# Seven block products in place of eight for six of 22 pairs of feature tiles in the down projections of a two-layer encoder

## The chip, the cores and the metric

The kernel runs on one core of a Trainium2 chip. The metric is the device time of one execution in microseconds. The profile is one execution, recorded by the hardware profiler; its rows give the time of each instruction on each engine: PE (TensorE, matmuls), DVE (VectorE), ACT (ScalarE), POOL and SP (the queue that issues DMAs).

## The reference

Two layers over 256 tokens of width 2048. Each layer has a token mixer (attention) and a gated channel mixer, each between two RMS norms, with a residual: x = x + norm_post(f(norm_pre(x))). All in float32. The part that matters here is the channel mixer:

```python
u = h @ w_up                                  # 256 x 2048 by 2048 x 11264
gate = depthwise_conv3(u[..., :5632]) + b
return (gelu(gate) * u[..., 5632:]) @ w_down  # 256 x 5632 by 5632 x 2048
```

The last product is the down projection. It runs twice, once per layer.

## The kernel before

**Numbers in two parts.** Every float32 operand of a matmul is kept as a high and a low part in the type fp32r. A product of two tiles is three matmuls, high by high, high by low and low by high (`mm3`, lines 172 to 174). The stationary operand holds 128 features by 128 tokens, the moving one 128 features by 512 outputs.

**Weights.** All weights are one list of tiles of 128 x 1024 (512 KB), in the order of their use (`all_chunks`); a tile of a down projection holds two feature tiles by 512 outputs, so the 44 feature tiles make 22 pairs. `_load` (line 103) fetches a tile through SP's DMA queue into one of four buffers, `_split` makes its parts: ScalarE copies into `whi` (line 117), VectorE subtracts into `wlo` (line 118); each of these has three buffers. `weights()` is called once for each tile as its products are issued: it splits two tiles ahead and loads three further.

**The down projection.** `out_proj` (the part ahead of line 364) goes through four groups of 512 outputs. In a group, `proj_tok` sums 22 weight tiles into two PSUM banks, one per half of 128 tokens; one weight tile is an item of 12 matmuls (2 halves x 2 feature tiles x 3). After a group, ScalarE squares and sums each half (line 282) for the norm, and VectorE multiplies it by the gain into `m` (line 350). The last group keeps back three weight tiles (`HOLD`) and finishes the first half of the tokens before the second, so that the first half's part of what follows can begin: `factor` (lines 374 to 379) forms each token's factor, `add` (line 383) adds the result to the residual `x`; in layer 0, transposes (line 405), dummy matmuls (`warm`, line 156) and the splitting of the new x for the next mixer follow, and in layer 1 the output transfers (line 396). In front of the down projection, the last group of the up projection is evacuated by lines 247, 248, 922, 923, 511 and 512 on ScalarE and VectorE; `gh` and `gl` hold the 44 feature tiles in two parts.

**What sets the order.** The kernel is written as a sequence with generators: `now(gen)` queues small pieces, `tick()` after each item issues one piece of each, `finish(gen)` issues the rest at once. The builder (a framework that puts in all waits) then gives each engine one fixed sequence, in which an instruction that it expects to be held up can be put behind a later one; instructions that write the same PSUM bank keep their order. On the chip each engine runs its sequence in order.

**Buffers by tag.** Tiles `xm0` to `xm3` hold the split x in the up projection (a quarter of the 16 feature tiles each, in this order) and later `m`.

## Time and profile before

| | us |
|---|---|
| runs (median of 3, lowest, highest) | 2072.59, 2072.4, 2081.38 |
| the profiled execution's own time | 2072.57 |
| its span, first to last instruction | 2070.8 |
| up projection of layer 0 (a stretch of it) | 560 to 820 |
| down projection of layer 0 | 823.05 to about 1062.6 |
| down projection of layer 1 | to about 2062.8 |

A row of the timeline is: start in us, duration in us, engine, line of the kernel, operation, output<-input, shapes, count; in brackets the idle time before it and what ended it. Matmuls are pipelined, so one of 389 ns can be followed by the next much sooner: the distance of two starts is the cost. The span is 1.8 us shorter than the execution's time.

### The profile page before, as it was taken

Reading aid. Unit: us, or ns where it says so; the run is one execution under the profiler, and the core shown is the slowest. Engines: PE = TensorE matmul, PEld = TensorE weight load, DVE = VectorE, ACT = ScalarE, POOL = GpSimd, SP = SyncE. Lnnn points to the kernel's source line nnn. Section 1 sums busy time; section 2 is a strip of 40 time slices with the busy share of each in tenths; the row PEclk is TensorE's granted clock in tenths of the full one; section 3 lists DMA queues with packets and bytes.
Section 4 is the critical chain, followed back from the end, with each engine's and each line's share of the span. In section 5 each row is a group of like instructions: output and inputs, shape, how many; then the busy total and the mean of one; then the engine's idle time right before and its main releaser. Section 6 shows DMA issues by size and latency. Waiting matters only on the chain.

```text
span 2070.8 us, 28951 instructions
## 1 busy us (share of the span) xinstructions
PE 2057.9 (99%) x10977; PEld 1764.1 (85%) x10977; DVE 1340.6 (65%) x2051; ACT 1084.6 (52%) x1695; POOL 0.2 (0%) x4
## 2 busy tenths in 40 slices
PE   9999999999999999999999999999999999999998
PEld 7888888888888888888888998888888888888886
DVE  6877757667667667444466875666766766754444
ACT  6655546555555555344455654555555555544443
POOL 0000000000000000000000000000000000000000
PEclk9999999999999999999999999999999999999999
DMA  8545565666666666666665445566666666666664
GB/s 315 176 153 163 164 200 174 186 193 190 188 192 191 187 192 190 196 198 199 198 186 170 125 129 177 177 188 190 185 195 191 188 191 190 185 200 198 198 194 154
DMA packets 108716, 385.96 MB, mean 186 GB/s; under 512 B 12064, under 2 KB 12576, under 8 KB 108576
## 3 DMA queue, kind: packets, MB, share of 16 engines
q1 hardware_dynamic: 108288, 383.83, 60.6%
q8 instruction: 86, 1.41, 0.3%
q14 instruction: 54, 0.44, 0.1%
q10 hardware_dynamic: 288, 0.28, 0.0%
HBM read 381.96 MB, written 2.10 MB: 185 GB/s over the span
## 4 chain that ended last, share of the span: by engine, by line
PE 98%; DVE 1%; ACT 0%; DMA 0%; issue 0%; DVEq 0%; SPq 0%
PE ps L186 31%; PE ps L172 16%; PE ps L174 16%; PE ps L173 16%; PE ps L187 16%; PE ps L463 1%; PE ps L242 1%; DVE x L383 1%; PE ps L405 0%; DMA raw<-in_w_in 0%; PE ps L790 0%; DVE wlo L118 0%; ACT junk L282 0%; PE ps L238 0%; DVE xhl L517 0%
## 5 line engine op out<-in xcount | busy, mean ns | idle before, releaser
L118 DVE TENSOR_TENSOR wlo<-raw,whi 128x1024 fp32r<-128x1024 f32 (+1 forms) x710 | 867.9, 1223 | 672.1 <-ACT whi L117 670.4
L117 ACT CAST whi<-raw 128x1024 fp32r<-128x1024 f32 (+1 forms) x710 | 745.9, 1052 | 786.5 <-PE ps L174 417.5
L186 PE MATMUL ps<-xhl,whi 128*128 128x512 f32 x2816 | 978.6, 394 | 1.0 <-DVE xhl L517 1.0
L187 PE MATMUL ps<-xhl,wlo 128*128 128x256 f32 x2816 | 779.2, 277 | 0.0
L186 PEld LDWEIGHTS ps<-xhl,whi 128*128 128x128 f32 x2816 | 527.6, 188 | 123.2 <-DVE xhl L517 1.9
L187 PEld LDWEIGHTS ps<-xhl,wlo 128*128 128x128 f32 x2816 | 528.7, 188 | 1.1 <-DVE wlo L118 0.5
L172 PE MATMUL ps<-whi,gh 128*128 128x512 f32 x704 | 273.9, 389 | 0.0
L174 PE MATMUL ps<-whi,gl 128*128 128x512 f32 x704 | 273.9, 389 | 0.0
L173 PE MATMUL ps<-wlo,gh 128*128 128x512 f32 x704 | 273.9, 389 | 0.0
L174 PEld LDWEIGHTS ps<-whi,gl 128*128 128x128 f32 x704 | 132.2, 188 | 27.7
L173 PEld LDWEIGHTS ps<-wlo,gh 128*128 128x128 f32 x704 | 132.2, 188 | 27.4
L172 PEld LDWEIGHTS ps<-whi,gh 128*128 128x128 f32 x704 | 132.2, 188 | 27.1
L172 PE MATMUL ps<-whi,xhl 128*128 128x512 f32 x352 | 138.8, 396 | 1.3 <-ACT whi L117 1.2
L173 PE MATMUL ps<-wlo,xhl 128*128 128x512 f32 x352 | 137.6, 391 | 0.0
L174 PE MATMUL ps<-whi,xhl 128*128 128x512 f32 x352 | 137.1, 391 | 0.0
L172 PE MATMUL ps<-whi,oh 128*128 128x512 f32 x256 | 100.0, 390 | 0.0
L173 PE MATMUL ps<-wlo,oh 128*128 128x512 f32 x256 | 99.7, 389 | 0.0
L174 PE MATMUL ps<-whi,ol 128*128 128x512 f32 x256 | 99.6, 389 | 0.0
L247 ACT COPY half<-ps 128x256 f32<-128x256 f32 x176 | 65.0, 369 | 45.6 <-PE ps L186 36.0
L172 PEld LDWEIGHTS ps<-whi,xhl 128*128 128x128 f32 x352 | 66.0, 188 | 15.1 <-ACT whi L117 1.5
L174 PEld LDWEIGHTS ps<-whi,xhl 128*128 128x128 f32 x352 | 66.0, 188 | 13.9
L173 PEld LDWEIGHTS ps<-wlo,xhl 128*128 128x128 f32 x352 | 66.3, 188 | 13.4 <-DVE wlo L118 0.9
(186 smaller groups left out, 1584.9 us busy)
## 6 DMA issues: line engine op xcount, KB each, us to landing
raw<-in_w_up SPq DMA_DIRECT2D x352, 512.0 KB, 4.1
raw<-in_w_down SPq DMA_DIRECT2D x176, 512.0 KB, 4.2
raw<-in_w_in SPq DMA_DIRECT2D x88, 512.0 KB, 3.8
raw<-in_w_out SPq DMA_DIRECT2D x64, 512.0 KB, 3.9
gb<-in_post SPq DMA_DIRECT2D x16, 256.0 KB, 3.9
raw<-in_w_qn SPq DMA_DIRECT2D x8, 512.0 KB, 3.6
raw<-in_w_kn SPq DMA_DIRECT2D x8, 512.0 KB, 3.6
raw<-in_w_v SPq DMA_DIRECT2D x8, 512.0 KB, 3.6
```

The source lines that it names most:

```text
L117: self.nc.scalar.copy(hi[:, s], raw[:, s])
L118: self.nc.vector.tensor_tensor(out=lo[:, s], in0=raw[:, s], in1=hi[:, s].bitcast(F32), op=ALU.subtract)
L172: mm(ps, lh, rh, start=start, stop=False)
L173: mm(ps, lh, rl, start=False, stop=False)
L174: mm(ps, ll, rh, start=False, stop=stop)
L186: mm(out[i], hi[:, s], x(k), start=k == 0, stop=False)
L187: mm(out[i][:, :T], lo[:, s], x(k)[:, :T], start=False, stop=k == nk - 1)
L242: self.tc.keep_in_program_order(self.nc.tensor.transpose(out, x, self.ident))
L247: self.nc.scalar.copy(b, ps[:, T:])
L383: return nc.vector.scalar_tensor_tensor(out=x, in0=m[c][:, t, s], scalar=r[t], in1=x, op0=ALU.mult, op1=ALU.add)
L463: nc.tensor.matmul(ps[:, i, :], l, r, start=n == 0, stop=n == len(pairs) - 1))
```

## The change

`ffn` calls a new function `down` in place of `out_proj`. It goes through the outputs in two halves of 1024 (two blocks of 512) in place of four groups of 512, so four PSUM banks take the sums of a half (two blocks by two token halves). Of the 22 pairs of feature tiles, 16 are done as before ("plain"), an item for each block. The first six pairs go by the Strassen-Winograd rule: two token halves, two feature tiles and two output blocks are a 2 x 2 by 2 x 2 block product, done with seven block products in place of eight. They come in four items (steps 0 to 3 with 2, 2, 2 and 1 products); the order of a half is four plain items, then for each such pair the steps 0, plain, 1, 2, plain, 3, plain, then the remaining ten plain items.

- Products that are shared between outputs go into four further PSUM banks. After the sixth pair `added` combines them, and `total` adds the result to the plain banks.
- The token sums of the rule (`sums` in `down`) are made on VectorE from the two parts of the tokens, in three blocks of two pairs, and split again. They use `xm3` as scratch and `xm0` to `xm2` for the results; the split x now sits in `xm0`, `xm1`, `xm3`, `xm2` in this order. What of them is not yet issued is issued ahead of the first step 0.
- The weight sums (`Seven.sums`) are four subtractions on VectorE for each pair and half, in place, issued right behind the split of step 0. Steps 0 and 1 split the one tile before and after, step 2 the other, step 3 a half tile.
- `passage` is the former end of `out_proj`; for the down projection `total` of the last block comes ahead of the squares there.

The diff, cut:

```diff
--- before.py
+++ after.py
...
+XM = 0, 1, 3, 2
+PAIRS = 6
+PLAIN0 = 4
+def down_order():
+    plain = [("plain", p, o) for o in range(2) for p in range(PAIRS, KF // 2)]
+    out, plain = plain[:PLAIN0], deque(plain[PLAIN0:])
+    for p in range(PAIRS):
+        for j in (0, None, 1, 2, None, 3, None):
+            out.append(plain.popleft() if j is None else ("seven", p, j))
+    return out + list(plain)
+class Seven:
+    def __init__(self, a, b):
+        self.srcs, self.raw = (a, b), None
+    def load(self, model):
+        if self.raw is None:
+            self.raw = []
+            for src, tag in zip(self.srcs, "ab"):
+                raw = model.room.tile([P, 1024], F32, tag=f"seven_{tag}", name=f"seven_{tag}", bufs=1)
+                model.nc.sync.dma_start(out=raw, in_=src)
+                self.raw.append(raw)
+    def step(self, model, j):
+        a, b = self.raw
+        return (a, a, b, self.t2)[j] if j else a
+    def sums(self, model):
+        nc = model.nc
+        a, b = self.raw
+        self.t2 = model.room.tile([P, 512], F32, tag="seven_t", name="seven_t", bufs=1)
+        a0, a1, b0, b1 = a[:, :512], a[:, 512:], b[:, :512], b[:, 512:]
+        for out, x, y in ((a0, b0, a0), (self.t2, b1, a0), (a1, a1, self.t2), (b0, b1, b0)):
+            nc.vector.tensor_tensor(out=out, in0=x, in1=y, op=ALU.subtract)
...
+        if isinstance(self.chunks[i], tuple):
+            self.chunks[i][0].load(self)
+            self.loaded[i] = None
+            return
...
         raw = self.loaded.pop(i)
+        seven, step = self.chunks[i] if raw is None else (None, 0)
+        if seven:
+            raw = seven.step(self, step)
         hi = self.wp.tile([P, 1024], F32R, tag="whi", name="whi", bufs=3)
         lo = self.wp.tile([P, 1024], F32R, tag="wlo", name="wlo", bufs=3)
-        n = 1024 // parts
+        n = raw.shape[-1] // parts
         with self.behind(self.gate):
             for j in range(parts):
                 s = slice(n * j, n * j + n)
                 self.nc.scalar.copy(hi[:, s], raw[:, s])
                 self.nc.vector.tensor_tensor(out=lo[:, s], in0=raw[:, s], in1=hi[:, s].bitcast(F32),
                                              op=ALU.subtract)
+        if seven and step == 0:
+            seven.sums(self)
...
-            self.xhl[c] = self.act.tile([P, 4, 2, T], F32R, tag=f"xm{c}", name=f"xhl{c}")
+            self.xhl[c] = self.act.tile([P, 4, 2, T], F32R, tag=f"xm{XM[c]}", name=f"xhl{c}")
...
-        part = self.col("part", 2)
-        nc.vector.tensor_reduce(out=part, in_=ss[:, :, 0:3], op=ALU.add, axis=AX.X)
-        nc.vector.tensor_scalar(out=part, in0=part, scalar1=1.0 / D, scalar2=EPS, op0=ALU.mult, op1=ALU.add)
+        part = self.three(ss)
         ps = self.proj_tok(nk, parts, order, hold=HOLD)
         m.append(room.tile([P, 2, 512], F32, tag=tag, name="m3", bufs=bufs))
+        self.passage(m, part, lambda t: ps[t], lambda t: scaled(3, t), pre)
...
+            self.square_sums(acc, last_sum(t))
...
-            g = lambda k: (gh[k // 4][:, k % 4, :], gl[k // 4][:, k % 4, :])
-            return self.out_proj(KF, g, 2 * layer + 1, pre, (sp, "m3", 1))
+            self.down(gh, gl, 2 * layer + 1, pre)
+    def down(self, gh, gl, post, pre):
+        nc = self.nc
+        add = lambda out, a, b, op=ALU.add: nc.vector.tensor_tensor(out=out, in0=a, in1=b, op=op)
+        mm = self.mm3
+        ss = self.small.tile([P, 2, 4], F32, tag="ss", name="ss", bufs=2)
+        seven, m, gains = [], [], []
+        def sums():
+            for i in range(PAIRS // 2):
+                tmp = self.act.tile([P, 2, 1024], F32, tag="xm3", name="sums")
+                add(tmp[:, 0], gh[i].rearrange("p k t -> p (k t)").bitcast(F32),
+                    gl[i].rearrange("p k t -> p (k t)").bitcast(F32))
+                a = tmp[:, 0].rearrange("p (q k t f) -> p q k t f", q=2, k=2, t=2)
+                s = tmp[:, 1].rearrange("p (q n f) -> p q n f", q=2, n=4)
+                a11, a12, a21, a22 = (a[:, :, k, t] for t in range(2) for k in range(2))
+                add(s[:, :, 0], a21, a22)
+                add(s[:, :, 1], s[:, :, 0], a11, ALU.subtract)
+                add(s[:, :, 2], a11, a21, ALU.subtract)
+                add(s[:, :, 3], a12, s[:, :, 1], ALU.subtract)
+                yield
+                seven.append(self.act.tile([P, 2, 4, 2, P], F32R, tag=f"xm{i}", name=f"seven{i}"))
+                self.parted(seven[i][:, :, :, 0, :], seven[i][:, :, :, 1, :], s)
+                yield
+        def tokens(k, t):
+            return tuple(g[k // 4][:, k % 4, t * P:(t + 1) * P] for g in (gh, gl))
+        def summed(p, n):
+            return tuple(seven[p // 2][:, p % 2, n, i, :] for i in range(2))
+        def operands(kind, p, j, t):
+            if kind == "plain":
+                return [(2 * j + t, lambda k=2 * p + i: tokens(k, t), i) for i in range(2)]
+            if t:
+                return []
+            return [[(4, lambda: tokens(2 * p, 0), 0), (0, lambda: tokens(2 * p + 1, 0), 1)],
+                    [(5, lambda: summed(p, 0), 0), (1, lambda: tokens(2 * p + 1, 1), 1)],
+                    [(7, lambda: summed(p, 2), 0), (2, lambda: summed(p, 3), 1)],
+                    [(6, lambda: summed(p, 1), 0)]][j]
+        def added(h, at):
+            p1, p5, p6, p7 = at
+            x = m[h]
+            nc.scalar.copy(x[:, 0, 0], p1)
+            add(x[:, 1, 0], p6, x[:, 0, 0])
+            yield
+            add(x[:, 0, 1], p7, x[:, 1, 0])
+            add(x[:, 1, 0], p5, x[:, 1, 0])
+            yield
+            add(x[:, 1, 1], p5, x[:, 0, 1])
+            yield
+        def total(h, o, t):
+            x = m[h][:, o, t]
+            add(x, banks[2 * o + t], x)
+            return x
+        def scaled(h, o, t):
+            x = m[h][:, o, t]
+            add(x, x, gains[2 * h + o], ALU.mult)
+        def done(h, o, first=None):
+            if first:
+                yield from first
+            for t in range(2):
+                self.square_sums(ss[:, t, 2 * h + o:2 * h + o + 1], total(h, o, t))
+                yield
+                scaled(h, o, t)
+                yield
+        gains.append(self.gain_row(post, 0))
+        summing = self.now(sums())
+        items = down_order()
+        units = [n for n, item in enumerate(items) if item[0] == "seven"]
+        ended = None
+        for h in range(2):
+            if h == 0:
+                gains.append(self.gain_row(post, 1))
+            n = len(items) - (HOLD if h else 0)
+            todo = [(i, t) for i in range(n) for t in range(2)] + \
+                [(i, t) for t in range(2) for i in range(n, len(items))]
+            used = [(i, t, *op) for i, t in todo for op in operands(*items[i], t)]
+            first, last = {}, {}
+            for q, u in enumerate(used):
+                first.setdefault(u[2], q)
+                last[u[2]] = q
+            used = deque(enumerate(used))
+            banks = self.acc(4)
+            def products(i, t, w):
+                while used and used[0][1][:2] == (i, t):
+                    q, (_, _, b, x, blk) = used.popleft()
+                    c = slice(512 * blk, 512 * blk + 512)
+                    xh, xl = x()
+                    mm(banks[b], xh, xl, w[0][:, c], w[1][:, c], q == first[b], q == last[b])
+            for i in range(n):
+                if i == units[0]:
+                    self.finish(summing)
+                    banks += [self.psum("at") for _ in range(4)]
+                w = self.weights()
+                for t in range(2):
+                    products(i, t, w)
+                self.tick()
+                if i == units[-1]:
+                    m.append(self.act.tile([P, 2, 2, 512], F32, tag="xm2" if h else "xm3", name=f"m{h}"))
+                    if h:
+                        gains.append(self.gain_row(post, 3))
+                    ended = self.now(done(h, 0, added(h, banks[4:])))
+            if h == 0:
+                self.finish(ended)
+                gains.append(self.gain_row(post, 2))
+                ended = self.now(done(0, 1))
+                self.finish(ended)
+                self.table(AF.Sqrt, ss[:, 0, 1:2])
+        self.finish(ended)
+        part = self.three(ss)
+        ws = [self.weights(self.at + HOLD - j) for j in range(HOLD)]
+        for t in range(2):
+            for j in range(HOLD):
+                products(n + j, t, ws[j])
+        self.passage([x[:, o] for x in m for o in range(2)], part, lambda t: total(1, 1, t),
+                     lambda t: scaled(1, 1, t), pre)
...
+        def down(w):
+            items = []
+            for h in range(2):
+                pairs = [Seven(w[2 * h, p], w[2 * h + 1, p]) for p in range(PAIRS)]
+                items += [w[2 * h + j, p] if kind == "plain" else (pairs[p], j) for kind, p, j in down_order()]
+            return items
         ffn = lambda l: groups(a[f"w_up{l}"], [g for j in range(NFG) for g in (j, NFG + j)]) + \
-            groups(a[f"w_down{l}"], range(4))
+            down(a[f"w_down{l}"])
```

## Rows read from the trace of the kernel before

**Rows 1.** The page's part 1: busy time, share of the span, instructions.
```profile
PE 2057.9 (99%) x10977; PEld 1764.1 (85%) x10977; DVE 1340.6 (65%) x2051; ACT 1084.6 (52%) x1695; POOL 0.2 (0%) x4
```

**Rows 2.** The page's part 4: the chain that ended last, by line.
```profile
PE ps L186 31%; PE ps L172 16%; PE ps L174 16%; PE ps L173 16%; PE ps L187 16%; PE ps L463 1%; PE ps L242 1%; DVE x L383 1%; PE ps L405 0%; DMA raw<-in_w_in 0%; PE ps L790 0%; DVE wlo L118 0%; ACT junk L282 0%; PE ps L238 0%; DVE xhl L517 0%
```

**Rows 3.** Busy time by stretch: layer 0's down projection, then its up projection.
```profile
core 0: us, PE busy (x) PEld busy (x) DVE busy (x) ACT busy (x) POOL busy (x), PEclk, DMA share, GB/s
...
820.00:1058.00 238.00, 238.00 (x1056) 197.26 (x1056) 115.78 (x111) 99.43 (x109) 0.00 (x0) 1.00 0.65 196
560.00:820.00 260.00, 260.00 (x1502) 227.27 (x1502) 177.25 (x279) 139.45 (x208) 0.00 (x0) 1.00 0.63 190
```

**Rows 4.** Timeline in the middle of layer 0's down projection, all engines.
```profile
901.96 0.39 PE L172 MATMUL ps<-whi,gh 128*128 128x512 f32 x1
902.16 1.06 ACT L117 CAST whi<-raw 128x1024 fp32r<-128x1024 f32 x1 [1.67 <-PE ps L174]
...
903.25 1.22 DVE L118 TENSOR_TENSOR wlo<-raw,whi 128x1024 fp32r<-128x1024 f32 x1 [1.50 <-ACT whi L117]
...
904.68 0.39 PE L172 MATMUL ps<-whi,gh 128*128 128x512 f32 x1
```

**Rows 5.** Groups by line and shape: busy us, mean ns of one, idle before.
```profile
L118 DVE TENSOR_TENSOR wlo<-raw,whi 128x1024 fp32r<-128x1024 f32 x708 | 866.6, 1225 | 671.6 <-ACT whi L117 669.9
...
L117 ACT CAST whi<-raw 128x1024 fp32r<-128x1024 f32 x708 | 744.8, 1053 | 786.1 <-PE ps L174 417.5 <-PE ps L186 302.1 <-issue 49.3
...
L172 PE MATMUL ps<-whi,gh 128*128 128x512 f32 x704 | 273.9, 389 | 0.0
L174 PE MATMUL ps<-whi,gl 128*128 128x512 f32 x704 | 273.9, 389 | 0.0
L173 PE MATMUL ps<-wlo,gh 128*128 128x512 f32 x704 | 273.9, 389 | 0.0
...
L350 DVE TENSOR_TENSOR m<-ps,gb 128x512 f32<-128x512 f32 x32 | 22.0, 686 | 9.7 <-ACT junk L282 9.7
```

**Rows 6.** Timeline where layer 0's up projection ends and its down projection begins.
```profile
818.68 1.23 DVE L118 TENSOR_TENSOR wlo<-raw,whi 128x1024 fp32r<-128x1024 f32 x1 [1.55 <-ACT whi L117]
...
822.59 0.75 DVE L248 TENSOR_TENSOR u<-ps,half 128x256 f32<-128x256 f32 x2
...
823.05 0.39 PE L172 MATMUL ps<-whi,gh 128*128 128x512 f32 x1
...
824.60 1.22 DVE L118 TENSOR_TENSOR wlo<-raw,whi 128x1024 fp32r<-128x1024 f32 x1
...
825.73 0.76 DVE L512 TENSOR_TENSOR gl<-u,gh 128x256 fp32r<-128x256 f32 x2
...
830.21 1.22 DVE L118 TENSOR_TENSOR wlo<-raw,whi 128x1024 fp32r<-128x1024 f32 x1
```

**Rows 7.** Timeline of TensorE at the start of layer 1's mixer.
```profile
1066.33 0.39 PE L173 MATMUL ps<-wlo,xhl 128*128 128x512 f32 x1
1066.56 0.39 PE L172 MATMUL ps<-whi,xhl 128*128 128x512 f32 x1
1066.79 0.40 PE L174 MATMUL ps<-whi,xhl 128*128 128x512 f32 x1
```

**Rows 8.** Timeline of the end of layer 0's down projection.
```profile
1060.31 2.08 DVE L383 SCALAR_TENSOR_TENSOR x<-m,postr,x 128x512 f32<-128x512 f32 x3
...
1062.31 1.22 DVE L118 TENSOR_TENSOR wlo<-raw,whi 128x1024 fp32r<-128x1024 f32 x1
...
1062.64 0.60 ACT L282 ACTIVATE junk<-ps 128x512 bf16<-128x512 f32 x1 [1.67 <-PE ps L174]
```

**Rows 9.** Timeline of the end of layer 1's down projection.
```profile
2060.89 2.74 DVE L383 SCALAR_TENSOR_TENSOR x<-m,postr,x 128x512 f32<-128x512 f32 x4
...
2062.82 0.60 ACT L282 ACTIVATE junk<-ps 128x512 bf16<-128x512 f32 x1 [3.06 <-PE ps L174]
```

**Rows 10.** The page's part 6: DMA issues, count, size, us to landing.
```profile
raw<-in_w_down SPq DMA_DIRECT2D x176, 512.0 KB, 4.2
```

More of the change, by code (lines that the diff above doesn't have):

```diff
@@ L344, in gain_row @@
         def gain_row(c):
-            gb = self.small.tile([P, 512], F32, tag="gb", name="gb", bufs=2)
-            nc.sync.dma_start(out=gb, in_=self.a["post"][post:post + 1, 512 * c:512 * c + 512].broadcast_to([P, 512]))
-            gains.append(gb)
+            gains.append(self.gain_row(post, c))
         def scaled(c, t):
@@ L355, in out_proj @@
             ps = self.proj_tok(nk, parts, order, before if c == 0 else {})
-            m.append(self.act.tile([P, 2, 512], F32, tag=f"xm{c + 1}", name=f"m{c}"))
+            m.append(self.act.tile([P, 2, 512], F32, tag=f"xm{XM[c + 1]}", name=f"m{c}"))
             for t in range(2):
@@ L361, in out_proj, with gain_row, three, passage @@
                 self.table(AF.Sqrt, ss[:, 0, 1:2])
-        part = self.col("part", 2)
-        nc.vector.tensor_reduce(out=part, in_=ss[:, :, 0:3], op=ALU.add, axis=AX.X)
-        nc.vector.tensor_scalar(out=part, in0=part, scalar1=1.0 / D, scalar2=EPS, op0=ALU.mult, op1=ALU.add)
+        part = self.three(ss)
         ps = self.proj_tok(nk, parts, order, hold=HOLD)
         m.append(room.tile([P, 2, 512], F32, tag=tag, name="m3", bufs=bufs))
+        self.passage(m, part, lambda t: ps[t], lambda t: scaled(3, t), pre)
+    def gain_row(self, post, c):
+        gb = self.small.tile([P, 512], F32, tag="gb", name="gb", bufs=2)
+        self.nc.sync.dma_start(out=gb, in_=self.a["post"][post:post + 1, 512 * c:512 * c + 512].broadcast_to([P, 512]))
+        return gb
+    def three(self, ss):
+        part = self.col("part", 2)
+        self.nc.vector.tensor_reduce(out=part, in_=ss[:, :, 0:3], op=ALU.add, axis=AX.X)
+        self.nc.vector.tensor_scalar(out=part, in0=part, scalar1=1.0 / D, scalar2=EPS, op0=ALU.mult, op1=ALU.add)
+        return part
+    def passage(self, m, part, last_sum, scaled3, pre):
+        nc = self.nc
         r = []
@@ L388, in out_proj @@
         if pre is None:
-            scaled(3, 0)
+            scaled3(0)
             for t in range(2):
@@ L392, in out_proj @@
                     factor(1)
-                    scaled(3, 1)
+                    scaled3(1)
                 for c in range(4):
@@ L424, in pair @@
                 if c == 3:
-                    scaled(3, 0)
-                    scaled(3, 1)
+                    scaled3(0)
+                    scaled3(1)
                     add(c, 0, full)
@@ L896, in ffn @@
         with tc.tile_pool(name=f"ffn{layer}", bufs=1) as sp:
+            self.room = sp
             xs = self.xhl
@@ L924, in ffn @@
                     self.parted(gh[gi][:, i, :], gl[gi][:, i, :], u)
[L925 to L926 removed]
+            self.down(gh, gl, 2 * layer + 1, pre)
+    def down(self, gh, gl, post, pre):
+        nc = self.nc
+        add = lambda out, a, b, op=ALU.add: nc.vector.tensor_tensor(out=out, in0=a, in1=b, op=op)
[108 more added lines that the diff above has]
+                     lambda t: scaled(1, 1, t), pre)
```

1 line of the change is left out of this document (removed).

## The prediction

> **What bounds the kernel now.** Read the engines' shares first [rows 1]: TensorE is busy 99% of the span and VectorE 65%. The chain that ended last, by line, says the same of the path [rows 2]: matmul lines hold nearly all of it. The stage table then shows how the down projection of layer 0 differs from the up projection [rows 3]: TensorE is full in both, but VectorE is busy 115.8 of 238 us in the down projection against 177.25 of 260 us in the up projection. So a matmul taken out of the down projection is time taken off the path, as long as VectorE, which is half idle there, can feed what is left. The steady timeline gives the feeding in detail [rows 4]: one item (a 1024-wide weight tile, 12 matmuls) starts at 901.96 and the next at 904.68, so an item is 2.72 us and a matmul 2.72/12 = 0.2267 us. ScalarE starts its cast 0.20 us after an item starts (that is when the buffer of the item before comes free), VectorE's subtraction follows 1.09 us later, and the low part is done at 904.47, for an item that starts at 907.40. The slack is 2.9 us, and VectorE idles 1.50 us per item.
>
> **What it removes.** The 12 x 22 pairs x 4 groups are 1056 matmuls per layer; the groups of rows count 704 for each of three lines in both layers [rows 5], 2112. After the change a half has 16 plain pairs x 2 output blocks x 12 + 6 pairs x 7 products x 3 = 510, so 1020 per layer and 36 fewer. Over both layers 72 x 0.2267 = **16.3 us** goes, all of it on the path.
>
> One page speaks against that price. The Trainium skill, "TensorE: Matmul & The Clock Gate", section "Back-to-back issue gap", gives about 131 ns per matmul of 512 columns in a sustained stream; by it 72 matmuls are an estimated 9.4 us and the sum below ends 6.9 us later. The trace disagrees with its 226.7 ns, and the trace is used.
>
> **What it adds to VectorE and ScalarE inside the pairs.** A seven-pair with its three plain items lasts 57 matmuls, 12.92 us, on TensorE. VectorE's subtraction of a 1024-wide tile is 1.225 us long [rows 5], but the next independent one starts 1.13 us after it (824.60 to 825.73, [rows 6]). Six full splits at 1.13, one half split and four 512-wide subtractions at 0.686 each (nearest row: the 512-wide product, [rows 5]) make 10.2 of 12.92 us; ScalarE has 6 x 1.053 and one half, 6.9. On average that fits. The tight place is the plain item behind a pair's first step. Count from the start of the fourth step before it: 0.68 + 2.72 + 1.36 = 4.76 us later the plain item starts, and its second matmul, the first that needs a low part, at 4.99. VectorE meanwhile does the split of the next first step (ready at 0.20 + 1.09 = 1.29, through 2.42), the four subtractions written behind it (through 5.16), and only then that plain item's split, through 6.39. So it comes 1.4 us late, and TensorE can fill 0.2 of that with a matmul of the other token half. Bounds: 0 (the split is put between the subtractions, or other matmuls are put ahead) and 1.2 us for each of 22 pairs (the first pair of each layer is in the next term). The builder doesn't keep the written order: at 824.60 a split stands in the middle of an evacuation written ahead of it [rows 6], and where a low part is late at the start of the next mixer it has alternated the two token halves, L173, L172, L174 [rows 7]. So I take a value near the lower end, 0.2 us, **4.4 us** in all.
>
> A second page bears on the same row. The Trainium skill, "VectorE: DVE Perf Modes", section "The DRAIN you can't avoid", says that the next operation does not start until the pipe is empty; by it the pair costs an estimated 10.8 us of VectorE and the opening below ends 1.4 us later in each layer. The trace shows 1.13 against 1.225 and is used.
>
> **The opening of each down projection.** Before, VectorE is solid from 822.59 until 831.43 with the last evacuation and the splits through the fifth item [rows 6]; the first down matmul is at 823.05. New ahead of the first pair are the token sums: three blocks, each a 1024-wide addition (1.13), four 256-wide operations (0.375 each, two take 0.75, [rows 6]) and a 1024-wide split (1.13), 3.76 us, so 11.3 us; then the pair's four subtractions, 2.74, and the splits of the next three items, 3.4. In written order, with the sums all issued ahead of the split of the pair's second step, VectorE reaches the third step's split at 831.43 + 17.4 = 848.9. TensorE wants it at 823.05 + 4 x 2.72 + 1.36 + 2.72 + 1.36 = 839.4. That is 9.5 us late, the upper bound. The lower is 0: the blocks of pairs 2 to 5 (7.5 us) aren't needed yet, and the scratch tile is free about two items before the up projection ends, where VectorE idles 1.55 us per item [rows 6]; 848.9 - 7.5 - 2.7 = 838.7. The ends are far apart; the row that shows a split pulled forward speaks for the lower, the explicit finish of the sums for the upper. I take the middle, 5 us per layer, **10 us**.
>
> **The tail.** The last output block now needs an addition on VectorE (0.69) before its squares, for each token half. In layer 0 it pushes the three additions at 1060.31 by 0.73, the split at 1062.31 to 1063.04, and then the second half's own addition runs 1064.17 to 1064.86; the squares, at 1062.64 before [rows 8], start at 1064.90, 2.26 later. In layer 1 the four additions at 2060.89 go to 2061.62 and hold VectorE 2.66 us, the new one ends at 2064.96, and the squares at 2062.82 [rows 9] move by 2.18. Queued behind are the second half's factor, additions and output transfers, or the next mixer's first matmuls. **4.4 us**; 1.9 if the builder puts the new addition ahead of the split (+1.13) and of the additions (+0.73).
>
> **What costs nothing.** The weight transfers are as many as before; in a pair 5 x 0.5 MB in 12.92 us is 203 GB/s against 196 now [rows 3]. The two weight tiles of a pair are single-buffered, so the next pair's first load waits for the split of the second step and what is queued on SP waits with it; with 4.2 us to landing [rows 10] it is there 1.4 us before its split can start. If that cover goes, the loss falls in the pair term. The other block's recombination (8 extra additions per half) lies beside ten plain items, each with 1.5 us of idle VectorE [rows 4]. The first half's last evacuation covers itself: the second half begins in banks 0 and 1, already empty.
>
> **The sum.** -16.3 + 4.4 + 10 + 4.4 = +2.5 us on the profiled execution's 2072.57 us, which is also the median of the runs (2072.59): **2075 us**. A measurement of this kernel can tell about 0.5%, 10 us, from no change.
>
> **The rivals.** *The order is the written one* (slower). Then every pair's plain item waits behind the four subtractions, 1.2 us each: 22 x 1.2 = 26.4 in place of 4.4, 2097 us. For it: VectorE runs what is queued in order, and a queued subtraction can't be passed. Against: rows 6 and 7 show a builder that reorders where it foresees a wait. It decides from 0.56 us per pair on, where the total is 10.4 us over. Chance 0.27, at all prices from 0.56 to 1.2.
> *VectorE's slack hides everything* (faster). The sums start in the up projection's idle slots and the later blocks fall behind the splits, no pair waits: -16.3 + 4.4, or 1.9 with the shorter tails, 2058 to 2061 us. For it: 2.7 of 12.92 us are free in a pair, and half of VectorE everywhere else. Against: the sums all stand ahead of one split. It needs all waits together under 1.5 us, or under 4 with the shorter tails. Chance 0.22.
> *The saving isn't made*: were products issued eight to a pair, the three lines would count 2112 again. The counts above leave this next to no chance.
>
> **The numbers.** My forecast, a gain eaten by waits of VectorE so that the total stays within 0.5%, has 0.51. Its own range is 2064 to 2083. For 8 in 10 I add the nearer parts of both rivals: 2060 to 2090 (0.7 us per pair with the middle opening). The full bounds would be 2058 and 2106 (both openings at 9.5 and 1.2 per pair).
>
> **What would show it.** Right: 2040 matmuls on the three lines, still 0.2267 us apart; TensorE's idle time in the down projections rising from none to some 15 us, with most of it in the first 25 us of each, put down to the low-part subtraction; the squares of each tail some 2 us later behind the last matmul; VectorE near 80% busy in the pairs; the granted clock still 1.00. Wrong: matmuls in step through the opening (then the sums were hidden and the kernel is faster), or the same gap once per pair, at the plain item behind the first step (then it is slower).

## The result, and the profile after

The changed kernel takes **2079.95 us** (median of 20 runs, 2078.85 to 2097.52) against 2072.63 of the kernel before (20 runs in the same hours): ratio 1.004, 95% interval 1.0026 to 1.0054. The profiled execution took 2079.68 us, its span is 2077.9. A part of the executions of most kernels here, the one before among them, is about 9 or 18 us longer in the up projections, which the change doesn't touch (last section); so the table of the experiments gives the lowest run beside the median, and losses are read from the down projections alone.

Busy time by engine, the answer to [rows 1], and the two groups that answer to [rows 5] for line 172, now line 230 (lines 231 and 232 count the same):

```profile
PE 2052.2 (99%) x10905; PEld 1748.7 (84%) x10905; DVE 1477.6 (71%) x2263; ACT 1125.6 (54%) x1753; POOL 0.2 (0%) x4
...
L230 PE MATMUL ps<-whi,gh 128*128 128x512 f32 x584 | 226.7, 390 | 0.0
...
L230 PE MATMUL ps<-whi,seven 128*128 128x512 f32 x96 | 37.7, 427 | 9.2 <-ACT whi L173 9.2
```

3 x (584 + 96) = 2040 matmuls: the saving is made. The first down matmul of layer 0 starts at 822.67 and the last at 1063.93, of layer 1 at 1827.01 and 2067.24. 1019 steps of 0.22667 us are 230.98 us, so TensorE lost **10.3 us** in layer 0 and **9.3 us** in layer 1; the kernel before lost 0.02 in either. Busy time by stretch (as [rows 3]; then the opening of each layer, and one pair with its three plain items):

```profile
core 0: us, PE busy (x) PEld busy (x) DVE busy (x) ACT busy (x) POOL busy (x), PEclk, DMA share, GB/s
820.00:1058.00 238.00, 233.57 (x1010) 188.26 (x1009) 181.24 (x214) 120.03 (x138) 0.00 (x0) 0.99 0.61 190
835.00:840.00 5.00, 2.82 (x8) 1.76 (x7) 5.00 (x8) 2.94 (x3) 0.00 (x0) 0.83 0.15 34
840.00:845.00 5.00, 5.00 (x20) 3.97 (x19) 4.02 (x5) 1.67 (x3) 0.00 (x0) 0.83 0.76 269
1840.00:1845.00 5.00, 2.93 (x12) 2.19 (x13) 5.00 (x8) 2.94 (x3) 0.00 (x0) 1.00 0.28 71
...
882.60:896.02 13.42, 13.22 (x58) 10.55 (x57) 10.15 (x12) 6.60 (x8) 0.00 (x0) 1.00 0.62 198
```

Each opening has a hole in TensorE beside a solid VectorE. In layer 0 the granted clock falls too, and matmuls behind the hole start 0.43 us apart (TensorE's timeline there):

```profile
834.94 0.61 PE L230 MATMUL ps<-whi,gh 128*128 128x512 f32 x2
837.29 0.50 PE L230 MATMUL ps<-whi,seven 128*128 128x512 f32 x1 [1.73 <-ACT whi L173]
838.24 0.74 PE L230 MATMUL ps<-whi,seven 128*128 128x512 f32 x1 [0.45 <-ACT whi L173]
838.78 0.63 PE L231 MATMUL ps<-wlo,gh 128*128 128x512 f32 x1
839.21 0.63 PE L232 MATMUL ps<-whi,gl 128*128 128x512 f32 x1
```

By the gaps above 0.2267 the openings lost 4.3 and 3.0 us. The rest, 6.0 and 6.3 us, lies in the pairs but for some 0.9 us spread thinly over all steps: 18 pairs lose 0.48 to 0.52 us each, the second pair of each layer 0.9 and 1.2, the seventh, the first of the second half, nothing. One such loss (VectorE, ScalarE, TensorE):

```profile
862.62 1.22 DVE L174 TENSOR_TENSOR wlo<-seven_a,whi 128x1024 fp32r<-128x1024 f32 x1 [1.27 <-ACT whi L173]
863.76 1.22 DVE L174 TENSOR_TENSOR wlo<-raw,whi 128x1024 fp32r<-128x1024 f32 x1
864.90 0.68 DVE L76 TENSOR_TENSOR seven_a<-seven_b,seven_a 128x512 f32<-128x512 f32 x1
865.62 0.69 DVE L76 TENSOR_TENSOR seven_t<-seven_b,seven_a 128x512 f32<-128x512 f32 x1
866.23 0.69 DVE L76 TENSOR_TENSOR seven_b<-seven_b 128x512 f32<-128x512 f32 x1
866.83 0.68 DVE L76 TENSOR_TENSOR seven_a<-seven_a,seven_t 128x512 f32<-128x512 f32 x1
868.70 1.23 DVE L174 TENSOR_TENSOR wlo<-seven_a,whi 128x1024 fp32r<-128x1024 f32 x1 [1.19 <-ACT whi L173]
...
861.53 1.05 ACT L173 CAST whi<-seven_a 128x1024 fp32r<-128x1024 f32 x1 [1.44 <-PE ps L232]
...
867.62 1.05 ACT L173 CAST whi<-seven_a 128x1024 fp32r<-128x1024 f32 x1 [4.08 <-DVE seven_a L76]
868.58 1.05 ACT L173 CAST whi<-seven_b 128x1024 fp32r<-128x1024 f32 x1
...
868.59 0.39 PE L232 MATMUL ps<-whi,gl 128*128 128x512 f32 x1
868.81 0.41 PE L230 MATMUL ps<-whi,seven 128*128 128x512 f32 x1
869.06 0.40 PE L230 MATMUL ps<-whi,gh 128*128 128x512 f32 x1
869.68 0.74 PE L230 MATMUL ps<-whi,seven 128*128 128x512 f32 x2 [0.23 <-ACT whi L173]
870.26 0.40 PE L231 MATMUL ps<-wlo,seven 128*128 128x512 f32 x1
```

The builder put the plain item's subtraction (863.76) ahead of the four sums, so that item was in time. Late is **step 1**: its cast waits for the last of the four sums, 4.08 us of ScalarE's idle time, and its subtraction, 868.70 to 869.93, waits for that cast, with VectorE idle for 1.19. Step 1's first two matmuls need only the cast and start in step (868.81, 869.06). The builder put two high products of step 2 ahead of step 1's low ones, and they wait: TensorE's hole ends, here at 869.68 and in the other pairs alike, 0.05 us behind step 2's cast, which stands on ScalarE behind step 1's. It is a chain and not a full engine: VectorE is busy 10.15 of 13.42 us in a pair.

The builder also exchanged the last two sums. As written, the sum that step 1 still needs (`a1`) is the third; in all 24 pairs it ran as the fourth, here at 866.83. By the distances of these rows (0.72 us between two sums of which one needs the other, 0.11 from a sum's end to the cast) the written order would start both casts an estimated 0.5 us earlier, about the whole of a pair's loss. No run tests that by itself.

The end of layer 1 answers to [rows 9]: the new addition stands ahead of the squares in each token half (2063.59 and 2069.15), and the second half's squares start 2.62 us behind the last matmul (2067.24) where they started 0.42 behind it.

```profile
2063.59 0.69 DVE L1002 TENSOR_TENSOR m<-ps,m 128x512 f32<-128x512 f32 x1 [1.77 <-PE ps L232]
...
2066.49 2.74 DVE L454 SCALAR_TENSOR_TENSOR x<-m,postr,x 128x512 f32<-128x512 f32 x4
2069.15 0.68 DVE L1002 TENSOR_TENSOR m<-ps,m 128x512 f32<-128x512 f32 x1
...
2069.86 0.63 ACT L340 ACTIVATE junk<-m 128x512 bf16<-128x512 f32 x1 [4.50 <-DVE m L1002]
```

From the last down matmul to the next down projection's first (layer 0) takes 2.05 us more than before, to the end (layer 1) 2.27 more. The sum: -16.3 (matmuls) + 19.5 (lost) + 4.3 (tails) - 0.4 (first matmul earlier) = 7.1 us, the difference of the spans, 2077.9 - 2070.8.

### The profile page after: what moved, and what is told of

It is laid out like the page before. It is cut to its first block, busy times and chain, and to the rows that moved or that the text cites. A ratio compares the mean times of both kernels' runs of the same rounds, so it can differ in the third digit from the quotient of the medians.

```text
span 2077.9 us, 29115 instructions
## 1 busy us (share of the span) xinstructions
PE 2052.2 (99%) x10905; PEld 1748.7 (84%) x10905; DVE 1477.6 (71%) x2263; ACT 1125.6 (54%) x1753; POOL 0.2 (0%) x4
## 4 chain that ended last, share of the span: by engine, by line
PE 95%; DVE 3%; ACT 1%; issue 0%; DMA 0%; DVEq 0%; ACTq 0%; SPq 0%
PE ps L244 31%; PE ps L245 16%; PE ps L231 15%; PE ps L232 15%; PE ps L230 15%; PE ps L534 1%; PE ps L300 1%; ACT whi L173 1%; DVE x L454 1%; DVE wlo L174 1%; PE ps L476 0%; DMA raw<-in_w_in 0%; DVE sums L1002 0%; PE ps L861 0%; ACT junk L340 0%
## 5 line engine op out<-in xcount | busy, mean ns | idle before, releaser
L174 DVE TENSOR_TENSOR wlo<-raw,whi 128x1024 fp32r<-128x1024 f32 (+1 forms) x662 | 807.5, 1221 | 493.9 <-ACT whi L173 491.8
L173 ACT CAST whi<-raw 128x1024 fp32r<-128x1024 f32 (+1 forms) x662 | 694.2, 1050 | 614.4 <-PE ps L244 302.3
L231 PE MATMUL ps<-wlo,gh 128*128 128x512 f32 x584 | 228.2, 391 | 0.0
L232 PE MATMUL ps<-whi,gl 128*128 128x512 f32 x584 | 228.0, 390 | 0.0
L230 PE MATMUL ps<-whi,gh 128*128 128x512 f32 x584 | 226.7, 390 | 0.0
L231 PEld LDWEIGHTS ps<-wlo,gh 128*128 128x128 f32 x584 | 110.1, 188 | 23.4 <-DVE wlo L174 0.4
L230 PEld LDWEIGHTS ps<-whi,gh 128*128 128x128 f32 x584 | 110.0, 188 | 22.3
L173 ACT CAST whi<-seven_a 128x1024 fp32r<-128x1024 f32 x48 | 50.5, 1052 | 115.6 <-DVE seven_a L76 84.7
L174 DVE TENSOR_TENSOR wlo<-seven_a,whi 128x1024 fp32r<-128x1024 f32 x48 | 58.8, 1224 | 48.8 <-ACT whi L173 48.8
L230 PEld LDWEIGHTS ps<-whi,xhl 128*128 128x128 f32 x352 | 66.0, 188 | 14.1 <-ACT whi L173 0.9
```

The source lines that it names most:

```text
L173: self.nc.scalar.copy(hi[:, s], raw[:, s])
L174: self.nc.vector.tensor_tensor(out=lo[:, s], in0=raw[:, s], in1=hi[:, s].bitcast(F32), op=ALU.subtract)
L230: mm(ps, lh, rh, start=start, stop=False)
L231: mm(ps, lh, rl, start=False, stop=False)
L232: mm(ps, ll, rh, start=False, stop=stop)
```

## The experiments

"Lost" is the time from first to last down matmul less 0.22667 us for each step between. Ratios are to the kernel before on the same chip.

| kernel | median (lowest) us | ratio, 95% interval | lost, layers 0 and 1 | last matmul to end |
|---|---|---|---|---|
| changed | 2079.95 (2078.85) | 1.004, 1.0026 to 1.0054 | 10.3, 9.3 | 10.66 |
| e3 by 1024 alone | 2073.17 (2072.94) | 1.0004, 0.9992 to 1.0017 | 0.0, 0.0 | 8.39 |
| e4 no last total | 2077.61 (2077.03) | 1.0021, 1.0002 to 1.0041 | 10.1, 10.2 | 9.39 |
| e2 eight plain | 2078.8 (2077.68) | 1.0034, 1.0018 to 1.0049 | 7.9, 9.6 | 10.72 |
| e1 step 3 first | 2084.1 (2082.47) | 1.0056, 1.0039 to 1.0074 | 11.9, 10.4 | 10.67 |
| e10 order alone | 2090.16 (2087.02) | 1.0086, 1.0067 to 1.0105 | 12.7, 14.0 | 10.66 |
| e6 sums in two parts | 2101.41 (2100.69) | 1.0135, 1.012 to 1.0151 | 19.6, 20.9 | 10.67 |
| e8 token sums spread | 2092.99 (2092.56) | 1.0094, 1.008 to 1.0107 | 17.1, 14.9 | 10.73 |
| e9 shared by matmul | 2093.83 (2092.73) | 1.0107, 1.0088 to 1.0126 | 18.1, 16.3 | 8.42 |
| e11 two plain behind 0 | 2101.3 (2092.96) | 1.0124, 1.0094 to 1.0154 | 16.1, 16.8 | 10.66 |
| e12 same, two parts | 2075.47 (2073.95) | 1.0015, 0.9991 to 1.004 | 6.5, 6.9 | 10.67 |
| e13 and the opening | 2077.04 (2068.08) | 0.9997, 0.9976 to 1.0018 | 4.3, 3.9 | 10.73 |
| e14 all three | 2069.72 (2067.77) | 0.999, 0.9972 to 1.0007 | 5.0, 4.2 | 8.42 |

**The outputs by 1024, without the seven products.**

```diff
-PAIRS = 6
+PAIRS = 0
...
         def total(h, o, t):
-            x = m[h][:, o, t]
-            add(x, banks[2 * o + t], x)
-            return x
+            return banks[2 * o + t]
...
```

> The outputs by 1024 alone: no pair by seven products, so 2112 matmuls, no sums, no addition in the tail; the plain items of a half in the order of its two output blocks. Theory (all losses are from the seven products): the time of the kernel before, 2072.6 us within 1. Rival (part of the loss is the new order of banks, gain rows and evacuations): 2075 us or more, with gaps at the borders of the halves.

Nothing is lost in either layer; the median is 0.47 us above the kernel before's 2072.7. The new order of banks, gain rows and evacuations costs at most about that much, and nothing in the down projections.

**The tail.**

```diff
-        self.passage([x[:, o] for x in m for o in range(2)], part, lambda t: total(1, 1, t),
-                     lambda t: scaled(1, 1, t), pre)
+        self.passage([x[:, o] for x in m for o in range(2)], part, lambda t: banks[2 + t],
+                     lambda t: add(m[1][:, 1, t], banks[2 + t], gains[3], ALU.mult), pre)
```

> The changed kernel without the addition of the shared products to the last output block of each half layer's second half (the last 512 output columns lack what the six pairs give through the shared products). Theory (the tail's 2.05 and 2.27 us are that addition, queued ahead of the squares in each token half): 4.3 us less, 2075.6 us (2074.5 to 2077). Rival (the squares would wait for the banks or for the additions anyway): less than 1.5 us gained, 2078.5 us or more.

The second half's squares start at 2085.01, 0.42 us behind the last matmul (2084.59), as in [rows 9], so the 2.2 us by which they were late are that addition. The median, though, is only 2.3 us under the changed kernel's, and the two intervals overlap. In the one profiled execution layer 1's opening lost 4.1 us in place of 3.0, and the end came 1.0 us later behind the last addition than in the kernel before, that is in the output transfer. The mechanism holds in the rows; the gain per run came out at half of what was expected. (In e9, below, where TensorE makes this addition, both tails come back nearly whole.)

**The opening, first try.**

```diff
-PLAIN0 = 4
+PLAIN0 = 8
```

> The changed kernel with eight plain items ahead of the first pair in place of four, so four fewer at the end of each half. Theory (the opening's stalls are a backlog of VectorE: 11.3 us of token sums and 2.7 us of weight sums in items that leave it 1.5 us each): four more items give it 6 us, so the 4.3 and 3.0 us of the two openings fall to at most 1 us together, the granted clock does not fall in the first layer's opening, the pairs stay at 0.5 us each: 2074 us (2072 to 2076). Rival (the loss comes from all the sums being called for ahead of one split, wherever that stands): the same 7 us appear four items later, 2080 us (2078 to 2082).

In the main a miss: layer 0's opening lost 2.3 us and layer 1's 3.9, for the clock fell there (0.68 in the window 1850 to 1855). That is 6.2 us in place of 7.3, and the median lies where the rival had it. The second pair's extra loss went, the others stayed at 0.5. VectorE is still solid up to the first pair: one scratch tile serves all three blocks, and the builder put the third block among the first pair's weight sums.

**The pair, three misses.** The order of a pair's steps alone is changed in e1 (the first new line) and e10 (the second); e6 has e10's order, with two sums behind step 0 and the other two held behind the second plain item.

```diff
-for j in (0, None, 1, 2, None, 3, None):
+for j in (0, None, 3, None, 1, 2, None):
+for j in (0, None, 3, None, 1, None, 2):
...
+        if step == 0:
+            with self.behind([low]):
+                next(self.weight_sums, None)
```

> The work of the changed kernel with the steps of a pair in the order 0, plain, 3, plain, 1, 2, plain; step 1 stands 6.8 us of matmuls behind step 0 and no longer 4.1. Theory (a chain within the pair: step 0's split, the four weight sums in place, then step 1's cast and subtraction, too long for the one plain item that covers it): the half-wide step 3 needs only the second sum, so its split is done some 0.6 us ahead of its matmuls, and step 1 has the time of another plain item. The recurring gap of 0.5 us per pair goes, about 10 us in all: 2070 us (2067 to 2073). Rival (VectorE, near 80% busy in the pairs, is short of time in total, whatever the order): the gap stays about 0.5 us per pair and only moves, 2080 us (2077 to 2083).

> The same order of steps, 0, plain, 3, plain, 1, plain, 2, with the four weight sums together as in the changed kernel. Theory (burst): the plain item behind step 3 has its low part done about 0.24 us late, of which matmuls that need only the high part fill some; 0 to 0.25 us per pair, 2070 to 2076 us, between the changed kernel and the one with the sums in two parts. Rival (the time between steps 0 and 1 alone decides, the sums may come together): nothing is left of the loss, the same time as with the sums in two parts within 0.5 us.

> The changed kernel with the steps of a pair in the order 0, plain, 3, plain, 1, plain, 2, and the four weight sums in two parts: two behind the split of step 0, two held behind the subtraction of the second plain item; the opening as it was. Theory (a pair loses time because four sums and the splits around them come to VectorE in one burst, while a split can begin only about one item and a half ahead of its use; over the whole pair VectorE has time to spare): laid out by the durations of the trace every split is done before its matmuls, so the 0.5 us per pair goes, about 9.5 to 10 us in all; the openings stay at 7 us or more: 2070 us (2068 to 2073). Rival (VectorE is short of time in total): the 0.5 us stays, 2080 us.

Neither theory: none got faster, and the one that spreads the sums is the slowest. e10 and e6 are slower than the changed kernel clear of the intervals; e1's interval overlaps with the changed kernel's, but its two layers lost 2.7 us more. In e1 step 1 itself is in time (in the pair at 896 it starts in step at 900.19), but the same pair loses 0.6 us at step 3 and the plain item behind it. The waits of the three kernels (e1, e10, e6; us in total, times, longest) have lines that the changed kernel does not have at all:

```profile
ACT whi L173 <- DMA seven_a<-in_w_down: 35.3, 18, 2.6
```

```profile
ACT whi L173 <- DMA seven_a<-in_w_down: 38.9, 20, 2.4
...
DVE seven_a L76 <- DMA seven_b<-in_w_down: 5.5, 9, 1.6
```

```profile
ACT whi L177 <- DMA seven_a<-in_w_down: 46.7, 17, 3.0
...
DVE seven_a L79 <- DMA seven_b<-in_w_down: 5.2, 10, 1.1
```

A pair's two weight tiles have one buffer each. Step 1 frees the one and step 2 the other; moved towards the end of the pair they free it later, the next pair's load is issued later, and step 0's cast waits for it. Then the sums are late, and all behind them. In the changed kernel the load was in time, as the prediction said under "What costs nothing": the first tile's is issued 5.1 us (median) ahead of the cast and lands in 3.7. The new order used up that cover: in e1, e10 and e6 the cast starts 0.1 us behind the landing, 4.7, 4.8 and 3.7 us after the issue. It is a resource that my layout of VectorE's time alone had left out. A second buffer for each tile wasn't tried, so how much of the loss is the load's is not shown by itself; where steps 1 and 2 stand early again (e11 and e12 below), ScalarE's wait for the tile falls from 35 to 47 us to 2.5 and 12.0.

**The opening and the tail again, on top of e6.** e8 has eight plain items; block 2 of the token sums is held behind the splits, block 3 spread over two pairs, and nothing is finished ahead of the first pair. e9 adds the shared products by matmuls with the identity.

```diff
...
+                held = lambda: self.behind([self.low] if i else [])
...
-                    self.finish(summing)
+                    while not seven:
+                        self.tick()
...
```

```diff
...
+            for part_of in range(2):
+                nc.tensor.matmul(banks[2 + t], self.ident_r, shared[0][:, part_of, t], start=False, stop=False)
...
```

> The kernel with the sums in two parts, and in the opening eight plain items ahead of the first pair, the second block of token sums held behind one split after another, the third block spread over the items of the first two pairs, and no call to finish the sums ahead of the first pair. Theory (openings lose time by the backlog on VectorE and by nothing else): both openings lose under 1 us together and the granted clock stays 1.00 there; the kernel is 7 us under the one with the sums in two parts: 2061 to 2065 us, that is the 16.3 us of matmuls less the tail's 4.3. Rival (the first pair waits in any case, for its weights or its banks): 3 us or more stay in each opening, 2067 us or more.

> The kernel with the token sums spread, and the shared products of the last output block added by TensorE: two matmuls per token half with the identity put them into the bank ahead of its last three items, so no addition stands ahead of the squares. Theory (the tail's 4.3 us are that addition): the squares follow the last matmul as before the change; 8 matmuls at 0.2267 us cost 1.8 us and 4.3 us come back, 2.5 us under the kernel with the token sums spread: 2059 to 2062 us. Rival (the cast and split of the shared products, or the matmuls between the last items, make a new wait): no gain, or slower.

The totals still hold e6's waits for the pairs' loads (44.6 and 30.6 us of ScalarE's idle time in e8 and e9), but the openings can be read. In the window 820 to 860 of e8 TensorE is full, at clock 1.00:

```profile
820.00:860.00 40.00, 40.00 (x182) 33.09 (x181) 35.28 (x52) 20.50 (x26) 0.00 (x0) 1.00 0.56 175
```

So the opening was a backlog of VectorE in the order in which it stood, not a shortage: the same sums, spread over more items, lose 0.1 us in layer 0 and nothing in layer 1. e8 makes three changes at once: the four more items, which alone were not enough (e2), the spreading, and no sums finished ahead of the first pair; the last two are not told apart. In e9 the tails come back (last matmul to end 8.42, layer 0's last down matmul to layer 1's first 761.50 us against e8's 763.37), and as much goes again: 1.8 us of matmuls, and 1.0 and 1.4 more lost.

**The pair, with step 1 left early.** Two plain items stand directly behind step 0, with the sums together (e11), or two of them behind step 0 and two behind the first plain item (e12).

```diff
-for j in (0, None, 1, 2, None, 3, None):
+for j in (0, None, None, 1, 2, None, 3):
...
+        if step == 0:
+            with self.behind([low]):
+                next(self.weight_sums, None)
```

> The changed kernel with one line changed: the steps of a pair in the order 0, plain, plain, 1, 2, plain, 3, so that two plain items stand behind step 0 in place of one. Both weight tiles of a pair are free again behind step 2's split, as in the changed kernel, and the next pair's loads (4.2 to 4.6 us) have the third plain item and the next step 0's lead to land. Theory (the 0.5 us per pair is step 0's split, the sums, and step 1's cast and subtraction in series behind one plain item): 2.7 us more lie between, the loss goes or falls under 0.2 us, 10 us less in all, the openings as they were: 2070 us (2068 to 2074). Rival (the burst on VectorE: then the first plain item's low part, queued behind the four sums, comes late in place of step 1, as the prediction had it): 0.3 to 1.0 us per pair stay, 2077 to 2090 us.

> The same order, 0, plain, plain, 1, 2, plain, 3, with the four weight sums in two parts, the first two behind step 0's subtraction and the other two held behind the first plain item's. Theory (series and burst both count, and nothing else): by the durations of the trace every split is in time, no pair loses over 0.1 us, 2070 us (2068 to 2073). Rival (the single-buffered weight tiles: step 1's split comes some 0.4 us later than with the sums together, and so does the next load of its tile): a wait of ScalarE for the pair's first weight tile, or of VectorE for its second, shows up, 0.3 us per pair or more, 2076 us or more.

e11 is the rival's case, the prediction's own mechanism, and dearer than the rival had it (0.3 to 1.0 us per pair, 2077 to 2090 us). Here the builder put the four sums ahead of the plain item's subtraction, which starts at 903.17 and ends at 904.39, and TensorE has a hole of about that size:

```profile
900.63 0.69 DVE L76 TENSOR_TENSOR seven_a<-seven_b,seven_a 128x512 f32<-128x512 f32 x1
901.36 0.69 DVE L76 TENSOR_TENSOR seven_t<-seven_b,seven_a 128x512 f32<-128x512 f32 x1
901.97 0.68 DVE L76 TENSOR_TENSOR seven_b<-seven_b 128x512 f32<-128x512 f32 x1
902.57 0.68 DVE L76 TENSOR_TENSOR seven_a<-seven_a,seven_t 128x512 f32<-128x512 f32 x1
903.17 1.22 DVE L174 TENSOR_TENSOR wlo<-raw,whi 128x1024 fp32r<-128x1024 f32 x1
...
903.37 1.04 ACT L173 CAST whi<-seven_a 128x1024 fp32r<-128x1024 f32 x1 [0.35 <-DVE seven_a L76]
...
902.85 0.61 PE L230 MATMUL ps<-whi,gh 128*128 128x512 f32 x2
904.46 0.50 PE L230 MATMUL ps<-whi,seven 128*128 128x512 f32 x1 [0.99 <-ACT whi L173]
904.80 0.40 PE L231 MATMUL ps<-wlo,gh 128*128 128x512 f32 x1
```

The row at 904.46 names ScalarE because the builder filled in a high product of step 1, whose cast ends at 904.41; the plain item's low part, wanted at about 903.3, was done only 0.02 us before that. The hole recurs with 1.23 to 1.28 us in most pairs. e12 does the same work in the same order of items with only two sums ahead of that subtraction:

```profile
910.88 0.69 DVE L78 TENSOR_TENSOR seven_a<-seven_b,seven_a 128x512 f32<-128x512 f32 x1
911.61 0.69 DVE L78 TENSOR_TENSOR seven_t<-seven_b,seven_a 128x512 f32<-128x512 f32 x1
912.29 1.22 DVE L177 TENSOR_TENSOR wlo<-raw,whi 128x1024 fp32r<-128x1024 f32 x1
913.44 0.68 DVE L78 TENSOR_TENSOR seven_a<-seven_a,seven_t 128x512 f32<-128x512 f32 x1
...
913.57 0.50 PE L237 MATMUL ps<-wlo,gh 128*128 128x512 f32 x1
```

Most pairs lose 0.18 to 0.4 us, the second of each layer 0.6, and the median, 2075.47, lies between theory and rival. So a pair's loss hangs on where the sums stand on VectorE; its total work is the same in all of these. Of e12's rest, the rival has a part: the four pairs in which ScalarE waits longest for the tile (1.29 to 1.42 us, at 1012.57, 1026.17, 1879.13 and 1892.81) lose 0.59 to 0.73 us.

**Together.**

> The order 0, plain, plain, 1, 2, plain, 3 with the weight sums in two parts, and the opening of the kernel with the token sums spread (eight plain items first, the second block held behind the splits, the third spread over two pairs, no call to finish the sums). Theory (the two remedies act on different waits and add up): both openings lose under 0.3 us, each pair 0.2 to 0.4 us, so each down projection takes about 234 us from its first matmul to its last in place of 237.5 to 237.9 with the pairs alone mended; 7 us less than that, 2068 us (2066 to 2071). Rival (the third block's sums, moved beside the pairs, take the time there that the two parts had freed): the first two pairs lose 1 us or more each, 2071 us or more.

> The same, and the shared products of the last output block added by TensorE with the identity ahead of the last three items, so that no addition stands ahead of the squares of the tail. Theory (the three losses, pairs, openings and tails, are separate): the last matmul to the end is 8.4 us as before the change, the two tails give back 4.3 us for 1.8 us of matmuls, 2.5 us under the kernel without it: 2065.5 us (2063 to 2069), clearly under the kernel before by 0.2 to 0.45%. Rival (a tail of VectorE's that was hidden shows up in its place): no gain over the kernel without it.

Both openings are clean in e13 and e14, and the pair's gains stay: the remedies add up. The medians missed what was expected all the same (2077.04 for 2068, 2069.72 for 2065.5); the lowest run of e13 is 2068.08. e14's third remedy gave almost nothing. Its tail is 8.42, but the matmuls with the identity wait for the split of the shared products, which ends on VectorE behind the evacuation of the block before (TensorE's timeline of e14):

```profile
1049.72 0.61 PE L1148 MATMUL ps<-shared,ident_r 128*128 128x512 f32 x2
1051.30 0.50 PE L1148 MATMUL ps<-shared,ident_r 128*128 128x512 f32 x1 [0.97 <-DVE shared L590]
```

That is 1.24 us in each layer, and with the 1.8 us of matmuls about what came back (beside e13 2.3 us at the end and 1.6 between the layers). The lowest runs of e13 and e14, 2068.08 and 2067.77, lie 4.3 and 4.6 us under the lowest of the kernel before beside them (2072.35), some 0.2%; by the intervals neither is told apart from it. Both are under the changed kernel, whose interval begins at 1.0026.

## Why the prediction was right in the sum, and where its steps failed

It said 2075 us, no change within 0.5%, range 2060 to 2090. It is 0.35% slower and inside the range. That the total stayed so near is in part luck: the pairs cost 7.8 us more than their term (0.55 us each, almost the 0.56 from which the rival decides), and the opening 2.7 less. Two of the prediction's figures do not come out of its own terms: 0.7 us per pair with the middle opening makes 2086 and not 2090, and 0.5% under 2072.57 is 2062 and not 2064.

- **The saving** (-16.3): right, 2040 matmuls at 0.2267. No run here shows the 131 ns of the Trainium skill ("TensorE: Matmul & The Clock Gate", "Back-to-back issue gap"): the down projections step at 0.2267 us in all of them.
- **The pair term** (4.4, that is 0.2 us per pair): the step that failed. It measured 12.2 us, mostly 0.5 a pair (some 1.1 of it, the extra of the second pairs, belongs to the opening's backlog, since it went with e2), and the place was wrong. I had said that "the plain item behind a pair's first step" would be late behind the four subtractions, and that the builder would ease it by reordering. It did reorder, and put that item first; then the sums, and step 1's cast and subtraction, stood later by one subtraction, in series, with one plain item to cover them, and step 2's cast behind step 1's. I had asked only who is behind the sums on VectorE, not who needs their result. My upper bound was sound: with the sums ahead of the item, e11 pays 1.26 us, against 1.2.
- **The opening** (10): 7.3, of which some 1.4 is the slow clock in layer 0 (seven matmuls 0.2 us longer). The backlog was there (VectorE solid up to the hole, in e2 as well, and no hole in e8); that the call to finish the sums has no part in it isn't shown. Right was that the sums start in the up projection's idle slots. The first block's addition starts there in the changed kernel at 817.33.
- **The tails** (4.4): 4.3, by the mechanism named (the rows of e4; e9).
- **What costs nothing**: the single-buffered tiles cost nothing here, and the outputs by 1024 at most half a microsecond (e3); e1, e10 and e6 show what happens when the cover of the first goes.
- **The signs**: VectorE near 80% busy in a pair was 76%. "The granted clock still 1.00" was wrong, 0.83 in two windows. "Most of it in the first 25 us" was wrong as well: 12.2 of 19.5 us lie in the pairs. And TensorE's idle time was to be put down to the low-part subtraction; the rows put it down to ScalarE's cast (9.2 us in the group of line 230 above).
- **The rivals**: "the order is the written one" gave 1.2 us per pair, and a total above +0.5% from 0.56 on; the pairs came to 0.55 on average, with a shorter opening. "VectorE's slack hides everything" was possible for the openings (e8) and nearly for the pairs (e12), but not in the order as built.

## What to carry to other kernels

Where extra work on a second engine feeds the bound engine, its share of busy time says little: lay out each chain from the event that lets a split begin (a buffer freed two items earlier) to the use of its result, and ask both who is queued behind the new instructions and who needs what they make. Before moving a step to give one chain more time, check which buffer it frees and who reloads that; reorderings that looked free on VectorE cost up to 10 us per layer (e6, with the sums spread; 2.4 and 4.7 for the order alone, e10), with waits for a single-buffered tile that had not been there. More than half of a 16 us saving can be eaten by twenty half-microsecond waits that no share of busy time shows.

## What the runs showed of the hardware that I had not expected

**A stall can cost twice.** After 2.1 us without a start (834.94's second matmul to 837.29), and 0.95 us behind that, TensorE ran at its lower level, 1.2 GHz, for seven matmuls: 0.43 us between starts in place of 0.227, in layer 0 of the changed kernel; layer 1's hole of the same size had no such sequel. In e2 the clock fell in layer 1 alone, in e4 in both; what decides it is open. The Trainium skill, "TensorE: Matmul & The Clock Gate", section "Wait — 56ns, not 53.3ns?", gives 426.7 ns at N = 512 for the cold array, and the trace agrees; its 215.7 ns for the warm one is 11 under the 226.7 here.

**Dependent and independent sums.** The second sum, which needs the first, starts 0.72 us after it (864.90 to 865.62); the third to run, which does not need the second, 0.61 after it, at a duration of 0.69. The Trainium skill, "VectorE: DVE Perf Modes", section "The DRAIN you can't avoid", has the next operation wait for an empty pipe, and adds that one that is not held starts earlier; the trace shows the wait only where one sum needs the one just ahead. The prediction took the first half alone.

**The up projection runs in one of two rhythms.** Windows of 100 us in the middle of layer 0's up projection, of the kernel before and of e12:

```profile
600.00:700.00 100.00, 100.00 (x579) 87.41 (x578) 70.78 (x117) 54.28 (x83) 0.00 (x0) 1.00 0.63 189
```

```profile
600.00:700.00 100.00, 100.00 (x568) 86.67 (x567) 67.35 (x109) 53.48 (x82) 0.00 (x0) 1.00 0.63 186
```

Both are full at clock 1.00, yet one does 579 matmuls and the other 568, 2% fewer, about 9 us over a layer: layer 0's first down matmul starts at 823.05 in the one and at 831.86 in the other. The code of this stage is the same but for which buffer holds which quarter of the split x. The profiled executions have the slower rhythm in neither layer (the kernel before), in one (e14) or in both (e12). What chooses it is open.
